# The first two column pairs of an input projection by plain products of quarters instead of seven products

## The chip, the cores and the metric

The kernel runs on one core of a Trainium2 chip. The metric is the device time of one execution in microseconds (us). Before the change it is 2447.02 us, the median of 3 runs (2444.62 to 2449.98). The profile is of one further execution, which took 2455.27 us.

The engines are named as in the profile: PE (TensorE, matrix products), PEld (its weight loads), DVE (VectorE), ACT (ScalarE), POOL (GpSimd) and SP (SyncE, which here issues the DMAs). Each engine takes its instructions in the order in which the program lists them.

## What is computed

One encoder block on a sequence of 2048 tokens of width 1024. The part that matters here is the first step: a pre-norm and one combined projection, whose columns feed all branches.

```python
h = rms_norm(x, norm_pre_g)
proj = jnp.einsum('bsd,de->bse', h, w_in.astype(h.dtype))
split_points = [int(p) for p in np.cumsum(SPLIT_SIZES)[:-1]]
u_a, z_a, q, k, v, o, z_b, gates, g_a, g_b = jnp.split(proj, split_points, axis=-1)
...
merged = jax.nn.sigmoid(g_a + b_merge[0]) * p_a + jax.nn.sigmoid(g_b + b_merge[1]) * p_b
```

Here x is 2048 x 1024 and w_in is 1024 x 9232. Of the columns, 16 are gate columns (`gates`), the other 9216 are 72 column blocks of 128. A pooling mixer and a matrix memory follow, then three more projections; they aren't touched by the change.

## The kernel before

**Halves and pairs.** `phase1` (L407) does the projection. It runs over two halves of the sequence with 1024 tokens each (`HALF`), and in each half over 36 pairs of column blocks (`in_pairs`, L48). The first two pairs are `("ga", 0)` and `("gb", 0)`, columns whose results only pass a sigmoid with a bias (`pair_g`, L653).

**Seven products.** A half of x, transposed, is a matrix of 1024 channels by 1024 tokens. It is cut into four quarters: A11 and A12 are the first 512 tokens (block 0) with the first and the last four of the eight k-tiles of 128 channels, A21 and A22 the same of the last 512 tokens (block 1). A pair's weights are cut alike: B11 and B21 are the first column block, B12 and B22 the second. `strassen` (L369) computes the four output quarters with seven products of quarters, the Winograd form. For it, the operands are A11, A12, A22 and the sums S1 = A21 + A22, S3 = A11 - A21, S2 = S1 - A11 and S4 = A12 - S2; the weights are B11, B21, B22 and the differences T1 to T4. Sums and differences are formed on DVE.

**Each product in three.** Every operand is split into a high part (ACT, L92) and a low part (DVE or POOL, L96). `mm3` (L98) does high by high, high by low and low by high for each of four k-tiles, so a product of quarters is 12 products on PE of 128x128 by 128x512. The seven take 84.

**Operands.** `operands` (L212) fetches x (L225). In half 0 it also forms the norm: squares on ACT (L246), their sum over k-tiles on DVE (L248), the sum over channels on PE (L252, tile `ssqp`), `rstd_of` (L146: DVE, then a power on POOL, L151), and `rows_of` (L167), which spreads the result over the partitions by PE (L173, tile `rbp`) and copies it to `rb` by ACT (L180). `scale_h` (L191, on DVE) scales x in place. `put` splits a k-tile into the tiles of `hp`, one buffer for each of A11, A12, S2, S1, S3, A22, S4. `combos` (L196) splits A22 and forms and splits S1, S3 and S2; S4 comes last (L208).

**Weights.** `load_w` (L301) loads raw weights into `wr` (3 buffers), `prep_w` (L341) forms the differences (L350, `wt`, 3 buffers) and splits everything into `wc` (16 buffers; a split matrix takes two). In half 1, `again_w` (L306) reads back differences that half 0 has stored, from the third pair on.

**The start of a half.** For the first two pairs and the last, `edge` is true (L446, L479): the product A12 by B21 comes right behind A11 by B11, since both need block 0 alone. The first two pairs run two steps each, then the gate columns of block 0 follow (`gates`, L513); then come the rest of the operands, the remaining products of both pairs, and the gate columns of block 1, which are formed from S1 and A22. In half 1 the operands are listed early by a priority of 400 instructions (`NEXT`); the x tiles 3 and 7 are first fetched as one block each and later fetched again whole.

**Order.** A planner with a cost model fixes the order of the instructions of each engine before the run, by priorities and by the times that it expects; `high_priority` raises the instructions traced inside it. `issue_after(i)` makes an instruction come behind `i` in the queue of the engine of `i`; instructions on other engines are not bound by it. Results in PSUM have two banks for each of `bankA`, `bankB`, `bankC` and `tr`.

Of the kernel before, what the change touches and what calls it, by code (L numbers as in the profile page):

```python
# [13 lines left out]
P = 128  # L14
# [63 lines left out]
class Kernel:  # L78
    def __init__(self, ctx, tc, a):
        self.ctx, self.tc, self.nc, self.a = ctx, tc, tc.nc, a  # L80
        self.n = 0
        self.free = {}
# [6 lines left out]
    def split(self, hi, lo, x, hi_eng, lo_eng):  # L89
        nc = self.nc  # L90
        if hi_eng == "act":
            nc.scalar.activation(hi, x, AF.Copy)  # L92
        else:
            nc.vector.tensor_copy(hi, x)
        eng = nc.gpsimd if lo_eng == "pool" else nc.vector
        eng.tensor_tensor(lo, x, hi.bitcast(F32), op=ALU.subtract)  # L96
# [70 lines left out]
    def rows_of(self, half, b, out, psum):  # L167
# [3 lines left out]
        for i in range(4):  # L171
            col = half * 8 + b * 4 + i
            nc.tensor.matmul(  # L173
# [6 lines left out]
        nc.scalar.activation(out, ps, AF.Copy)  # L180
# [7 lines left out]
    def put(self, H, n, j, x, he, le):  # L188
        self.split(H[n][0][:, j, :], H[n][1][:, j, :], x, he, le)

    def scale_h(self, x, kt, rb):  # L191
        self.nc.vector.scalar_tensor_tensor(
# [3 lines left out]
    def combos(self, H, j, a11, a12, a21, a22):  # L196

        nc = self.nc
        self.put(H, "A22", j, a22, "act", LE22)
# [12 lines left out]
    def operands(self, half, H, hp, wc, pool, psum):  # L212
# [3 lines left out]
        X = {}  # L216

        def whole(kt):
            x = pool.tile([P, HALF], F32, tag="raw" if kt < 4 else "acc", name=self.nm("xT"))
            X[kt] = x[:, :BLK], x[:, BLK:]  # L220
            return x

        def fetch(x, kt, b, n=1):
            t0 = half * HALF + b * BLK
            nc.sync.dma_start(x, a["xT"][kt, :, t0 : t0 + n * BLK])  # L225

        def parts(pool, tag, n):
            return tuple(pool.tile([P, BLK], F32, tag=tag, name=self.nm("xT")) for _ in range(n))

        last = []  # L230
        rb = self.rows.tile([P, HALF], F32, tag="rb", name=self.nm("rb"))
        if half == 0:
            for kt in range(KT):
                if kt % 4 == 3:
                    X[kt] = parts(wc, "wc", 2)
                else:
                    whole(kt)
            with tc.high_priority():
                for b in range(2):
                    for kt in range(KT):  # L240
                        fetch(X[kt][b], kt, b)
                for b in range(2):
                    acc = None
                    for kt in range(KT):
                        sq = pool.tile([P, BLK], F32, tag="p", name=self.nm("sq"))
                        nc.scalar.activation(sq, X[kt][b], AF.Square)  # L246
                        if acc is not None:
                            nc.vector.tensor_tensor(sq, sq, acc, op=ALU.add)  # L248
                        acc = sq
                    ps = psum.tile([P, 4], F32, tag="tr", name=self.nm("ssqp"), bufs=2)  # L250
                    for i in range(4):
                        nc.tensor.matmul(  # L252
                            ps[:, i : i + 1], acc[:, i * P : (i + 1) * P], self.one_c, start=True, stop=True
                        )
                    ssq = pool.tile([P, 4], F32, tag="ssq", name=self.nm("ssq"), bufs=2)
                    last = self.rstd_of(ssq, ps, 0, b)
                    self.rows_of(0, b, rb[:, b * BLK : (b + 1) * BLK], psum)
# [3 lines left out]
            yield  # L261
        else:
            for b in range(2):
                self.rows_of(1, b, rb[:, b * BLK : (b + 1) * BLK], psum)
            for kt in range(KT):
                if kt % 4 == 3:
                    X[kt] = parts(pool, "p", 1)
                    fetch(X[kt][0], kt, 0)
                else:
                    fetch(whole(kt), kt, 0, 2)  # L270
        H.update(self.alloc_h(hp))
        for kt in range(KT):
            with ExitStack() as es:
                if kt > 0:
                    for i in last:
                        es.enter_context(tc.issue_after(i.ins))
                self.scale_h(X[kt][0], kt, rb[:, :BLK])
                self.put(H, "A11" if kt < 4 else "A12", kt % 4, X[kt][0], "act", ("dve", "pool")[kt % 2])
        yield
        ends = []  # L280
        for j in range(4):
            for kt in (j, 4 + j):
                if len(X[kt]) == 1:
                    x = whole(kt)
                    fetch(x, kt, 0, 2)
                    self.scale_h(x, kt, rb)
                else:
                    self.scale_h(X[kt][1], kt, rb[:, BLK:])
            end = self.combos(H, j, X[j][0], X[4 + j][0], X[j][1], X[4 + j][1])
            if half == 1 and j == 0:  # L290
                end()
            else:
                ends.append(end)
# [3 lines left out]
    def put_w(self, W, wc, n, x, le):  # L297
        W[n] = tuple(wc.tile([P, 4, P], F32R, tag="wc", name=self.nm(f"w{n}{p}")) for p in "hl")
        self.split(*W[n], x, "act", le)

# [40 lines left out]
    def prep_w(self, W, raw, wc, wt):  # L341
# [11 lines left out]
        if "B11" not in W:  # L353
            put("B11", b11, "pool")
            if self.edge:
                put("B21", b21, "pool")
        yield
# [11 lines left out]
    def strassen(self, H, W, psum, pool, out, n=BLK, swap=False):  # L369


        nc = self.nc
        bank = {
# [32 lines left out]

    def phase1(self):  # L407
# [1061 lines left out]
```

## Time and profile before

| | us |
|---|---|
| median of 3 runs | 2447.02 |
| the profiled execution | 2455.27 |
| its span | 2453.5 |
| PE busy | 2331.6 |
| DVE busy | 1535.1 |
| POOL busy | 1141.2 |
| ACT busy | 902.0 |

The span runs from the first to the last instruction of the profiled execution; the rest of its time lies around that. A busy share is an average over the whole span. A product's end is modelled and products overlap, so the pace of PE is read from the starts of consecutive products, not from their durations. Idle time in a row is followed by what ended most of it. Lines are those of the kernel; L92, L96 and L104 to L106 are in helpers, so their rows are told apart by the tiles.

### The profile page before, as it was taken

How to read it: one execution, taken by the hardware profiler on the slowest of the kernel's cores; microseconds unless marked ns; L12 is line 12 of the kernel's file. 1: busy time of each engine (PE TensorE's matmuls, PEld its weight loads, DVE VectorE, ACT ScalarE, POOL GpSimd, SP SyncE). 2: the span in 40 equal slices, each digit the busy share in tenths (PEclk: the TensorE clock that was granted, in tenths of full speed). 3: DMA queues.
4: the chain of work that ended last, by engine and by line, in shares of the span. 5: the costliest groups of instructions: out<-in, count | busy, mean ns of one | idle time of the engine just before them, and what ended most of it. 6: DMA issues, size and time to landing. Idle time of an engine off the chain costs nothing. (4 is left out here: it accounts for less than half of the span.)

```text
span 2453.5 us, 35614 instructions
## 1 busy us (share of the span) xinstructions
PE 2331.6 (95%) x12517; PEld 2003.5 (82%) x12517; DVE 1535.1 (63%) x2540; ACT 902.0 (37%) x1781; POOL 1141.2 (47%) x902
## 2 busy tenths in 40 slices
PE   5899999999999889999999999998999999999898
PEld 3688788778778678888888888898989999999676
DVE  8787767796884655633554633887885333334885
ACT  5444433333434423321321323766664212111332
POOL 4556655565555423544454531444554211234675
PEclk9999999999999999999999999999999999999999
DMA  4456665555675366687767876767666546567443
GB/s 144 138 207 227 237 230 216 203 185 204 213 253 193 127 170 211 209 263 235 241 225 236 260 250 226 234 203 230 201 183 205 178 153 202 185 199 246 157 155 120
DMA packets 295874, 500.12 MB, mean 204 GB/s; under 512 B 26512, under 2 KB 139280, under 8 KB 295696
## 3 DMA queue, kind: packets, MB, share of 16 engines
q1 hardware_dynamic: 295696, 497.85, 61.6%
q8 instruction: 98, 1.61, 0.3%
q14 instruction: 80, 0.66, 0.1%
HBM read 308.49 MB, written 189.27 MB: 203 GB/s over the span
## 5 line engine op out<-in xcount | busy, mean ns | idle before, releaser
L565 DVE SCALAR_TENSOR_TENSOR acc<-raw,conv_w,acc 128x1022 f32<-128x1022 f32 (+1 forms) x128 | 212.1, 1677 | 13.0 <-ACT acc L561 12.4
L96 POOL TENSOR_TENSOR wB21l<-wraw,wB21h 128x512 fp32r<-128x512 f32 x76 | 115.3, 1517 | 188.0 <-ACT wB21h L92 131.0
L96 POOL TENSOR_TENSOR wB22l<-wraw,wB22h 128x512 fp32r<-128x512 f32 x76 | 109.7, 1443 | 113.1 <-ACT wB22h L92 82.6
L1117 POOL TENSOR_TENSOR qs<-q,isc 128x256 f32<-128x256 f32 x120 | 91.5, 766 | 138.0 <-PE num L1133 60.6
L841 PE MATMUL pb<-oxs,w_proj_mlstmh 128*128 128x256 f32 x512 | 143.7, 281 | 0.5 <-DVE sgb L1263 0.5
L843 PE MATMUL pb<-oxs,w_proj_mlstml 128*128 128x256 f32 x512 | 143.8, 281 | 0.0
L842 PE MATMUL pb<-oxs,w_proj_mlstmh 128*128 128x256 f32 x512 | 143.7, 281 | 0.0
L842 PE MATMUL paps<-pys,w_proj_poolh 128*128 128x256 f32 x512 | 143.1, 282 | 0.3 <-POOL pys L96 0.3
L841 PE MATMUL paps<-pys,w_proj_poolh 128*128 128x256 f32 x512 | 142.0, 282 | 0.3 <-DVE sga L970 0.3
L843 PE MATMUL paps<-pys,w_proj_pooll 128*128 128x256 f32 x512 | 141.9, 282 | 0.0
L96 POOL TENSOR_TENSOR wB11l<-wraw,wB11h 128x512 fp32r<-128x512 f32 x72 | 106.3, 1477 | 64.4 <-ACT wB11h L92 50.6
L104 PE MATMUL bankB<-A22h,wT4h 128*128 128x512 f32 x288 | 116.8, 405 | 17.6 <-DVE u L397 12.7
L397 DVE TENSOR_TENSOR u<-bankB,p 128x512 f32<-128x512 f32 x80 | 54.7, 683 | 117.4 <-PE bankB L106 117.4
L570 POOL TENSOR_TENSOR acc<-acc,raw 128x1022 f32<-128x1022 f32 (+1 forms) x32 | 82.9, 2590 | 91.0 <-ACT raw L569 76.2
L104 PE MATMUL bankB<-S3h,wT3h 128*128 128x512 f32 x288 | 114.3, 397 | 10.5 <-DVE u L393 10.5
L104 PE MATMUL bankC<-S1h,wT1h 128*128 128x512 f32 x288 | 113.6, 395 | 8.6 <-ACT S1h L92 7.1
L105 PE MATMUL bankA<-A11l,wB11h 128*128 128x512 f32 x288 | 114.2, 396 | 7.6 <-DVE A11l L96 6.0
L92 ACT ACTIVATE wB21h<-wraw 128x512 fp32r<-128x512 f32 x76 | 47.7, 628 | 195.3 <-PE bankA L105 87.1
L104 PE MATMUL bankB<-S2h,wT2h 128*128 128x512 f32 x288 | 112.8, 393 | 6.5 <-ACT S2h L92 6.5
L104 PE MATMUL bankA<-A12h,wB21h 128*128 128x512 f32 x288 | 113.3, 393 | 3.6 <-ACT p L386 3.6
L105 PE MATMUL bankB<-S2l,wT2h 128*128 128x512 f32 x288 | 113.4, 394 | 2.8 <-DVE S2l L96 2.8
L104 PE MATMUL bankC<-S4h,wB22h 128*128 128x512 f32 x288 | 112.9, 392 | 2.5 <-DVE u L635 2.5
(355 smaller groups left out, 7738.7 us busy)
## 6 DMA issues: line engine op xcount, KB each, us to landing
wraw<-in_w_in SPq DMA_DIRECT2D x112, 512.0 KB, 4.1
wt<-wT2h SPq DMA_DIRECT2D x34, 256.0 KB, 4.0
wt<-wT2l SPq DMA_DIRECT2D x34, 256.0 KB, 4.1
wt<-wT1h SPq DMA_DIRECT2D x34, 256.0 KB, 4.6
wt<-wT1l SPq DMA_DIRECT2D x34, 256.0 KB, 3.7
wt<-wT3h SPq DMA_DIRECT2D x34, 256.0 KB, 4.6
wt<-wT3l SPq DMA_DIRECT2D x34, 256.0 KB, 4.1
wt<-wT4h SPq DMA_DIRECT2D x34, 256.0 KB, 2.1
```

Of the source, the lines that this page charges most:

```text
L92: nc.scalar.activation(hi, x, AF.Copy)
L96: eng.tensor_tensor(lo, x, hi.bitcast(F32), op=ALU.subtract)
L104: nc.tensor.matmul(ps, wh, xh, start=start and kt == 0, stop=False, skip_group_check=True)
L105: nc.tensor.matmul(ps, wh, xl, start=False, stop=False, skip_group_check=True)
L397: nc.vector.tensor_tensor(u3, bank["B"], p1, op=ALU.add)
L565: nc.vector.scalar_tensor_tensor(acc[:, :n], raw[:, tap : tap + n], self.cw[:, ct, tap : tap + 1], acc[:, :n], op0=ALU.mult, op1=ALU.add,)
L570: nc.gpsimd.tensor_tensor(acc[:, :n], acc[:, :n], raw[:, :n], op=ALU.mult)
L841: nc.tensor.matmul(ps, wh, xh, start=i == 0, stop=False)
L842: nc.tensor.matmul(ps, wh, xl, start=False, stop=False)
L843: nc.tensor.matmul(ps, wl, xh, start=False, stop=i == n)
L1117: nc.gpsimd.tensor_tensor(qs[d], q[:, :, ck], isc[:, d, j % 2, None, :].to_broadcast([P, 2, P]), op=ALU.mult)
```

## The change

**Plain products for two pairs.** For the first two pairs of each half, `strassen` hands over to the new `quarters`. It takes the four output quarters one block at a time: for block u it has two banks, one for each column block, and adds up over the eight k-tiles three products for each bank. The two pairs and the gate columns advance together, a k-tile at a time. No sum and no difference is used. The last four banks go through `pair_g`'s `out` with nothing to add.

```diff
+    def quarters(self, H, W, psum, out):
+        nc = self.nc
+        for u, tags in enumerate(self.plain):
+            bank = [psum.tile([P, BLK], F32, tag=f"bank{t}", name=self.nm(f"bank{t}"), bufs=2) for t in tags]
+            for kt in range(KT):
+                xh, xl = (t[:, kt % 4, :] for t in H[f"A{u + 1}{1 + kt // 4}"])
+                es = ExitStack()
+                if u == 0 and kt == KT - 2 and self.half == 0:
+                    es.enter_context(self.tc.issue_after(self.ready[0].ins))
+                for e in range(2):
+                    wh, wl = (t[:, kt % 4, :] for t in W[f"B{1 + kt // 4}{1 + e}"])
+                    first, end = kt == 0, kt == KT - 1
+                    nc.tensor.matmul(bank[e], wh, xh, start=first, stop=False, skip_group_check=True)
+                    nc.tensor.matmul(bank[e], wl, xh, start=False, stop=False, skip_group_check=True)
+                    nc.tensor.matmul(bank[e], wh, xl, start=False, stop=end, skip_group_check=True)
+                es.close()
+                if kt < KT - 1:
+                    yield
+            with self.tc.issue_after(self.ready[1].ins):
+                for e in range(2):
+                    out(2 * u + e, bank[e], None)
+            yield
```

`ready` holds the last product of `rows_of` on PE and its copy to `rb` on ACT. So in half 0 the products of k-tile 6 of block 0 come behind block 1's `rbp` on PE, and the evacuations behind block 1's `rb` on ACT.

**Operands.** The blocks of x are fetched one behind the other, in half 0 with three raw weight loads between them. Tiles 3 and 7 of x lie in `wc`, which grows from 16 to 20 buffers, so nothing is fetched twice. All four quarters are split; A21 uses the buffer of S4. The norm of block 1 (`sums(1)`) is listed between k-tiles 1 and 2 of block 0's scaling, its instructions on DVE behind the second scaling, without a raised priority. The scaling of k-tile pairs is pinned behind the low part of the pair before. Two extra products (`busy`) go to PE in half 0 behind the sums of block 0.

```diff
+        def busy(w, x):
+            ps = psum.tile([P, BLK], F32, tag="bankC", name=self.nm("busy"), bufs=2)
+            nc.tensor.matmul(ps, w, x, start=True, stop=True)
...
+        scaled, lower = [], []
+        for b in range(2):
             for kt in range(KT):
+                if half == 0 and b == 0 and kt == 2:
+                    with tc.issue_after(scaled[1].ins):
+                        sums(1)
+                with ExitStack() as es:
+                    if kt > 0 and b == 0:
+                        for i in last if kt < 2 else lower[kt - 2 - kt % 2 :][:1]:
+                            es.enter_context(tc.issue_after(i.ins))
+                    scaled.append(self.scale_h(X[kt][b], kt, rb[:, b * BLK : (b + 1) * BLK]))
+                    lower.append(
+                        self.put(H, f"A{b + 1}{1 + kt // 4}", kt % 4, X[kt][b], "act", ("dve", "pool")[kt % 2])
+                    )
+            self.scaled = scaled
+            yield
+        ends = [self.combos(H, j, X[j][0], X[4 + j][0], X[j][1], X[4 + j][1]) for j in range(4)]
         yield
+        H.update(self.alloc_h({"S4": hp["S4"]}))
         for end in ends:
             end()
```

**The start of a half.** Both pairs' weights are split as they are, in four matrices each (`plain_w`). The sums S1 to S4 are now for the pairs from the third on. Their instructions on ACT are pinned behind the last evacuation of block 0; the differences of the third pair's weights, in half 0, are pinned on DVE behind the first scaling of block 1.

```diff
+                both = []
+                for i in range(2):
+                    self.plain = ("AB", ("CC", "AB")[i])
+                    both.append(work(i, W[i]))
+                    next(both[i])
+                self.plain = None
                 gates = self.gates(half, H, wg, psum, pool)
+                for _ in range(KT):
+                    next(gates, None)
+                    for g in both:
+                        next(g)
+                with tc.issue_after(self.evac.ins):
+                    next(ops)
...
                         if half == 0:
-                            run(self.prep_w(W, load(i), wc, wt))
+                            with tc.issue_after(self.scaled[8].ins) if i == 2 else ExitStack():
+                                self.prep_w(W, load(i), wc, wt)
```

**Gate columns.** Block 1's are formed from A21 and A22 with the weights as they are, so the difference of the gate weights goes; all eight k-tiles are split at once. The number of gate products, 16 for a block, stays.

200 lines of the change are left out of this document (87 added, 113 removed).

## The prediction

> **What bounds the kernel now.** I read the page first: its span, the row of TensorE (PE) and the row of its busy share in 40 slices. Then I cut the start into windows of 20 us.
>
> ```profile
> span 2453.5 us, 35614 instructions
> PE 2331.6 (95%) x12517; PEld 2003.5 (82%) x12517; DVE 1535.1 (63%) x2540; ACT 902.0 (37%) x1781; POOL 1141.2 (47%) x902
> PE   5899999999999889999999999998999999999898
> ```
>
> ```profile
> 0.00:20.00 20.00, 4.23 (x18) 3.88 (x18) 10.58 (x43) 11.91 (x19) 1.73 (x5) 1.00 0.84 274
> 20.00:40.00 20.00, 11.64 (x32) 8.09 (x32) 19.94 (x20) 8.57 (x16) 15.08 (x10) 0.96 0.27 84
> 40.00:60.00 20.00, 15.91 (x61) 9.76 (x59) 20.00 (x27) 11.79 (x19) 9.94 (x6) 0.95 0.24 80
> 60.00:80.00 20.00, 11.62 (x34) 7.04 (x35) 20.00 (x22) 7.65 (x13) 12.17 (x8) 0.74 0.01 3
> ```
>
> PE is busy 95% of the span and full from the third slice on, so the end of the kernel moves when work is taken from PE or a hole in PE is closed. In the windows (busy us and count for PE, PEld, DVE, ACT, POOL, then granted clock, DMA share, GB/s) the first 80 us are the hole: DVE has no idle time from 20 to 80 us while PE runs a third of what it could. VectorE, preparing operands, sets the pace there.
>
> How much is lost? The timeline gives PE's full pace (12 products lie between these two starts); the windows and the groups by line give what was done:
>
> ```profile
> 87.66 0.39 PE L104 MATMUL bankA<-A11h,wB11h 128*128 128x512 f32 x1
> 90.38 0.39 PE L104 MATMUL bankB<-A22h,wT4h 128*128 128x512 f32 x1
> ```
>
> ```profile
> 0.00:84.70 84.70, 47.86 (x160) 32.10 (x160) 73.04 (x114) 41.83 (x69) 41.18 (x30) 0.92 0.32 104
> 800.00:840.00 40.00, 29.83 (x109) 19.81 (x108) 34.50 (x38) 17.69 (x30) 21.66 (x15) 0.87 0.24 77
> ```
>
> ```profile
> L173 PE MATMUL rbp<-ident,rstd 128*128 128x128 f32 x16 | 4.2, 441 | 3.1 <-POOL rstd L151 3.1
> L252 PE MATMUL ssqp<-one_c,sq 128*128 128x1 f32 x16 | 3.7, 353 | 13.4 <-DVE sq L248 13.4
> ```
>
> Pace: (90.38 - 87.66)/12 = 0.227 us. By 84.7 us PE had done 160 records, of which 32 are the small ones of L173 and L252: 128 products, worth 29.1 us. **Half 0 is 84.7 - 29.1 = 55.6 us behind** a PE that never waits; from there on it runs without a gap for a while. At the start of half 1, 109 products fell into 40 us: 40 - 24.7 = **15.3 us behind**. The waits of PE name why:
>
> ```profile
> PE bankA L105 <- DVE A11l L96: 6.0, 2, 4.1
> PE bankB L104 <- ACT S2h L92: 3.5, 1, 3.5
> PE bankB L105 <- DVE S2l L96: 2.8, 1, 2.8
> ...
> PE bankC L104 <- ACT S1h L92: 6.9, 2, 5.9
> ```
>
> The first three are of the first 130 us, the last is of 800 to 840 us. Three of the four are waits for S1 or S2, the sums of quarters which only the seven-product scheme needs.
>
> **The change, part by part.**
>
> *More products.* A pair by seven products has 7 x 12 = 84, by plain products 8 x 12 = 96. Two pairs in each half: 24 more, 24 x 0.227 = 5.45 us a half. The 32 gate products of a half stay 32. Nothing hides this: PE is the bound.
>
> *Half 0: work for PE before the sums exist.* The two pairs and the gates now need only the scaled quarters, 224 products or 51 us. The chain to the first operand stays as it is:
>
> ```profile
> 13.13 1.87 PE L252 MATMUL ssqp<-one_c,sq 128*128 128x1 f32 x8 [13.13 <-DVE sq L248]
> 15.69 3.88 DVE L248 TENSOR_TENSOR sq<-sq,sq 128x512 f32<-128x512 f32 x5
> 15.74 1.53 POOL L151 TENSOR_TENSOR rstd<-ssq,half_c 128x4 f32<-128x4 f32 x1 [15.30 <-DVE ssq L149]
> 17.32 2.08 PE L173 MATMUL rbp<-ident,rstd 128*128 128x128 f32 x8 [2.32 <-POOL rstd L151]
> 20.06 0.75 DVE L192 SCALAR_TENSOR_TENSOR xT<-xT,norm_pre_g,rb 128x512 f32<-128x512 f32 x1 [0.50 <-ACT rb L180]
> 21.53 0.80 PE L104 MATMUL bankA<-A11h,wB11h 128*128 128x512 f32 x1
> 22.42 1.75 DVE L96 TENSOR_TENSOR A11l<-xT,A11h 128x512 fp32r<-128x512 f32 x1
> ```
>
> So PE starts its products at 21.5 us, as now. The two new "busy" products are not in this trace. By L173, 8 records of 128 columns take 2.08 us; one product of 512 columns (two records, four times as wide) is then 2 x 4 x 0.26 = 2.1 us. The first lies in the gap 15.0 to 17.3, the second between 19.4 and 21.5: bounds 0 and 4.2 us, taken as 0, since each gap is as long as it. POOL now has weight splits (1.47 us) queued before rstd, which may push the chain by up to one of them; that is in the stalls below.
>
> *Can the operands keep up?* One k-tile feeds 14 products, 3.2 us at full pace. The mean durations between 20 and 84 us (between 12 and 84 us for POOL):
>
> ```profile
> L192 DVE SCALAR_TENSOR_TENSOR xT<-xT,norm_pre_g,rb 128x512 f32<-128x512 f32 x16 | 16.2, 1060 | 0.5 <-ACT rb L180 0.5
> L203 DVE TENSOR_TENSOR xT<-xT,xT 128x512 f32<-128x512 f32 x4 | 4.6, 1215 | 0.0
> L202 DVE TENSOR_TENSOR xT<-xT 128x512 f32<-128x512 f32 x3 | 4.1, 1402 | 0.0
> L201 DVE TENSOR_TENSOR xT<-xT,xT 128x512 f32<-128x512 f32 x4 | 3.7, 953 | 0.0
> L96 DVE TENSOR_TENSOR S2l<-xT,S2h 128x512 fp32r<-128x512 f32 x4 | 3.7, 945 | 0.0
> ...
> L96 POOL TENSOR_TENSOR A11l<-xT,A11h 128x512 fp32r<-128x512 f32 x2 | 3.4, 1718 | 0.0
> L96 POOL TENSOR_TENSOR wB11l<-wraw,wB11h 128x512 fp32r<-128x512 f32 x2 | 2.9, 1466 | 3.4 <-ACT wB11h L92 3.4
> ```
>
> Two k-tiles cost DVE two scalings and one low part, about 3 us, and POOL one low part, 1.7 us, against 6.4 us of PE. Hence PE stays fed. DVE's list until the second quarter sum S2 is whole: 16 scalings 16.2, 8 low parts 8, 7 additions of squares at 0.78 to 1.75 (5.5 to 12, taken 7), gate weights 2, weight differences for the third pair 5, L201 3.7, L202 5.5 for four, L203 4.6, S2l 3.7: 56 us, from 20 to 76 us. PE asks for S2 after 224 + 12 products: 21.5 + 53.6 + 2 (cold clock, next) = 77. It is just in time; S4, eight operations later on DVE, is wanted 14 us later still. POOL's list to the same point, from 15 us on, is shorter: 13 weight splits at 1.47, 16 low parts at 1.72, two rstd at 1.53, 50 us, to 65.
>
> *The clock.* The first products run at half pace until PE has been full for a while:
>
> ```profile
> 39.04 0.80 PE L105 MATMUL bankA<-A11l,wB11h 128*128 128x512 f32 x1 [4.14 <-DVE A11l L96]
> 40.06 0.63 PE L104 MATMUL bankA<-A11h,wB11h 128*128 128x512 f32 x1
> 41.34 0.63 PE L104 MATMUL bankA<-A11h,wB11h 128*128 128x512 f32 x1
> 41.77 0.49 PE L105 MATMUL bankA<-A11l,wB11h 128*128 128x512 f32 x1
> 74.59 0.80 PE L105 MATMUL bankB<-S2l,wT2h 128*128 128x512 f32 x1 [2.77 <-DVE S2l L96]
> 79.45 0.43 PE L104 MATMUL bankB<-S2h,wT2h 128*128 128x512 f32 x1
> ```
>
> Three products from 40.06 to 41.34: 0.427 us each, and the full pace 2.7 us after 39.04 and 4.9 us after 74.59. At half pace a share of 1 - 0.227/0.427 = 0.47 is lost, so warming costs 1.3 to 2.3 us; taken 2.
>
> *Other stalls in half 0*, taken at 6 us: the first low part (0.9 to 2.7 us after the first product in the rows above), POOL's queue before k-tiles 4 to 7, the second block's sums (rbp is pinned ahead of k-tile 6), and S2. Below 0 isn't possible; the upper end is the rivals'. Half 0 is then behind by 21.5 + 2 + 6 = 29.5 us: 55.6 - 29.5 - 5.45 = **20.6 us gained**.
>
> *Half 1.* Block 0 works while the S4 buffer (now A21 too) is still read by half 0's last products; block 1 has 25 us of PE work as cover, and the third pair's sums 51 us. The second fetch of two x tiles, behind the 5.9 us wait for S1h, is gone since X keeps its tiles in the wider weight pool. I leave 3 us of the 15.3: 15.3 - 3 - 5.45 = **6.9 us gained** (bounds: 9.9 with no stall, 0 if 10 us stay).
>
> *DMA and SP.* The second block of x now queues behind three weight loads of 512 KB: 1.5 MB at the 274 GB/s of the first window, 5.7 us later. Now its squares and its rstd end so:
>
> ```profile
> 13.44 4.51 ACT L246 ACTIVATE sq<-xT 128x512 f32<-128x512 f32 x7 [0.33 <-DMA xT<-in_xT]
> 25.52 1.46 POOL L151 TENSOR_TENSOR rstd<-ssq,half_c 128x4 f32<-128x4 f32 x1 [1.90 <-DVE ssq L149]
> ```
>
> The squares would end near 23.7 instead of 18.0 us, still 19 us before k-tile 6 is issued (21.5 + 2 + 84 x 0.227 = 42.6). The evacuations pinned behind rb, and the sums' copies pinned behind the last evacuation of block 0, wait on ACT, which is under two thirds full in every window above; behind them on ACT stand only later splits. Cost 0; without that cover about 0.5 us each (8.57/16 in the second window).
>
> **Sum:** 20.6 + 6.9 = 27.5 us. Against the profiled execution's own 2455.3 us that is 2427.8; that execution stands 8.3 us above the median 2447.0 of the runs, so the forecast is 2447.0 - 27.5 = **2419.5, say 2420 us**.
>
> **Rivals.**
>
> 1. *PE is held at the pinned place.* If DVE does all of block 0 (8 scalings 8.1, 4 low parts 4, gates 2) before the 7 additions at 1.75 (12.3), these end at 46.5; with the sum on PE 1.9, POOL's queue and rstd 3.2, rbp 2.1 the place opens at 54, 11 us after 42.6, and PE cools: 2 more. Beyond my allowance that is 10 us: gain 17, 2430 us. For it: SP's new order delays these squares. Against: now the same chain is through at 27.0 (25.52 + 1.46). Chance 0.13.
>
> 2. *The clock stays at half pace through block 0.* Between 21.5 and 39 us PE is half busy and never speeds up; if the new start is as broken, 112 products at 0.427 end at 69.3 instead of 55: gain 13, 2434 us. Against it: 14 products a k-tile at half pace are 6 us, more than DVE needs, so PE would be full, which warmed it in at most 4.9 us above. Chance 0.1. The Trainium skill ("TensorE: Matmul & The Clock Gate", Part 1) says that the array runs at half clock until about 3.4 us of sustained activity and falls back after an idle window of that length. The 2.7 and 4.9 us above agree; by its figure my term of 2 us would be 1.6, an estimate, and any hole of over 3.4 us between blocks would cost that again.
>
> 3. *The sums are late after all.* With every two-input operation at 1.75 us, as A11l at 22.42, DVE's list takes 36 x 1.75 + 16.2 + 2 = 81 us and ends at 101, 24 us after S2 is wanted; of my allowance 2 us were for that, and PE cools once more, 2 us. Gain 3.5, 2443.5 us, no change that can be told. Against it: the means 0.95 to 1.4 us in the rows above. Chance 0.1.
>
> 4. *The rest of the phase pays.* The weight pool grows from 16 to 20 buffers and the order of the other 34 pairs of each half is planned anew; weight splits may run ahead of the evacuations on DVE for which PE already waits:
>
> ```profile
> PE bankB L104 <- DVE u L397: 11.9, 8, 4.3
> ```
>
> That is 1.5 us a wait, 8 times in the pairs from 95 to 1500 us. If most of the 34 pairs of half 0 had one (24 x 1.5 = 36 us), the kernel would be slower: 2447 - 27.5 + 36 = 2456; it decides from 22 such waits (27.5 + 4.9 = 32.4 us). Against it: the raw and difference buffers (3 and 3) stay and hold the planner back as now. Chance 0.08.
>
> That the change doesn't do what it says is excluded for the main step: the sums read scaled quarters, so they can't come ahead of them.
>
> **How the numbers follow.** Forecast 0.59, rivals 0.13, 0.1, 0.1, 0.08. The low end is all allowances gone: 20.6 + 6 + 6.9 + 3 = 36.5, so 2411; the high end takes in rivals 1 to 3: 2444. A measurement here tells 0.2%, 4.9 us, from no change. Faster by more: forecast and rivals 1 and 2, 0.82; within: rival 3, 0.1; slower: rival 4, 0.08.
>
> **What would show it.** Right: PE without a gap over 3 us from 21.5 to about 80 us, the clock full by 28 us, some 115 more products done by 84.7 us ((84.7 - 29.5)/0.227 = 243 against 128), no wait for S1h or S2h over 2 us in either half. Wrong: a wait of PE for rstd (L151) or rbp near 43 us (rival 1), products 0.427 us apart past 30 us (rival 2), a wait for S2h or S2l near 77 us (rival 3), more waits for L397 between 100 and 700 us (rival 4).

## The result, and the profile after

The changed kernel takes 2437.41 us (median, 2430.06 to 2438.41) where the kernel before takes 2447.02: a ratio of 0.995 with a 95% interval of 0.9939 to 0.9962, so 9 to 15 us less. The forecast was 2420 us, 27.5 us less. The sign is right; more than half of the gain is missing. The profiled execution of the changed kernel took 2438.41 us.

The page of the changed kernel, its span, the busy times and PE's row of slices:

```profile
span 2436.6 us, 35625 instructions
...
PE 2335.1 (96%) x12569; PEld 2008.3 (82%) x12569; DVE 1505.3 (62%) x2495; ACT 894.3 (37%) x1773; POOL 1148.2 (47%) x902
...
PE   7999899999999999999999999998999999999898
```

The first slice went from 5 to 7, and the dent in slices 14 and 15 (the start of half 1) is gone. A new 8 stands in slice 5, at 244 to 305 us, where the change touches nothing. The windows say how much (columns as in the prediction: busy us and count for PE, PEld, DVE, ACT, POOL, then granted clock, DMA share, GB/s):

```profile
0.00:81.20 81.20, 64.11 (x260) 47.96 (x261) 60.72 (x89) 41.16 (x67) 43.76 (x33) 0.96 0.36 122
81.20:105.00 23.80, 18.04 (x65) 13.74 (x64) 19.64 (x23) 10.94 (x20) 14.84 (x10) 0.86 0.71 255
800.00:840.00 40.00, 40.00 (x176) 31.21 (x175) 29.44 (x32) 19.45 (x36) 26.41 (x16) 1.00 0.34 114
```

The third pair begins at 81.2 us. Of the 260 records before that, 36 are the small ones and the busy ones, so 224 products: PE is 81.2 - 224 x 0.227 = 30.4 us behind, where it was 55.6 us behind. At the start of half 1, 176 products fill all 40 us: nothing is left of 15.3 us. Both are what the prediction's sum needed. But the second row is new. The kernel before ran this stretch without a hole:

```profile
81.20:105.00 23.80, 23.47 (x104) 19.09 (x103) 14.03 (x16) 9.81 (x17) 12.11 (x9) 1.00 0.61 202
```

Now it holds 65 products instead of 104, and 23.8 - 65 x 0.227 = 9.0 us are lost as soon as the new start is over. A third place is the long middle of half 0. Its window, first of the kernel before, then of the changed one:

```profile
105.00:790.00 685.00, 663.76 (x2911) 543.68 (x2910) 513.61 (x562) 263.30 (x427) 388.69 (x238) 0.99 0.61 217
```

```profile
105.00:790.00 685.00, 656.93 (x2869) 537.07 (x2868) 508.54 (x556) 258.34 (x420) 384.96 (x236) 0.98 0.60 214
```

PE does 42 products less in the same 685 us: 9.5 us. The ends of the projection come from the last S4 product in the listing of tile wB22h (first and last start stand behind the durations), before and after:

```profile
L104 PE MATMUL bankC<-S4h,wB22h x288: 387/389/628, 94.0 to 1520.5; 128*128 128x512 f32 x144
```

```profile
L105 PE MATMUL bankC<-S4h,wB22h x272: 389/389/500, 111.8 to 1506.7; 128*128 128x512 f32 x136
```

| of the profiled executions | before, us behind | after, us behind | difference |
|---|---|---|---|
| start of half 0, to the third pair | 55.6 | 30.4 | -25.2 |
| third pair, 81.2 to 105 us | 0.2 | 9.0 | +8.8 |
| middle of half 0, 105 to 790 us | 24.2 | 33.7 | +9.5 |
| start of half 1 | 15.3 | 0 | -15.3 |
| 48 more products of 0.227 us | | | +10.9 |
| sum | | | -11.3 |
| measured at the end of the projection | 1520.5 | 1506.7 | -13.8 |

The 55.6 us are counted to 84.7 us; by 81.2 us they are 55.1, so the sum is uncertain by 0.5 us. The 2.5 us left over lie in the rest of half 1, where the changed kernel does 11 products more between 840 and 1500 us. The spans differ by 16.9 us, but the profiled execution of the kernel before was one of its longest; by the ratio the gain is 12.2 us. The table names two losses that the forecast did not have, 8.8 and 9.5 us. The experiments are about these two.

### The profile page after: what moved, and what is told of

It reads as the page before. It is cut to its first block, busy times and chain, and to the rows that moved or that the text cites. A ratio compares the mean times of both kernels' runs of the same rounds, so it can differ in the third digit from the quotient of the medians.

```text
span 2436.6 us, 35625 instructions
## 1 busy us (share of the span) xinstructions
PE 2335.1 (96%) x12569; PEld 2008.3 (82%) x12569; DVE 1505.3 (62%) x2495; ACT 894.3 (37%) x1773; POOL 1148.2 (47%) x902
## 4 chain that ended last, share of the span: by engine, by line
PE 51%; DMA 10%; DVE 6%; issue 2%; POOL 1%; ACT 1%; SPq 0%; DVEq 0%; POOLq 0%; ACTq 0%
PE bankB L105 5%; PE bankB L107 5%; PE bankB L106 4%; PE num L1167 4%; PE bankC L105 3%; PE bankC L107 3%; PE bankC L106 3%; PE bankA L107 3%; PE bankA L106 3%; PE bankA L105 3%; PE paps L876 2%; PE paps L877 2%; PE paps L875 2%; DMA negM<-nm 1%; DVE o L1392 1%
## 5 line engine op out<-in xcount | busy, mean ns | idle before, releaser
L599 DVE SCALAR_TENSOR_TENSOR acc<-raw,conv_w,acc 128x1022 f32<-128x1022 f32 (+1 forms) x128 | 212.4, 1688 | 10.9 <-ACT acc L595 8.8
L97 POOL TENSOR_TENSOR wB22l<-wraw,wB22h 128x512 fp32r<-128x512 f32 x76 | 115.6, 1521 | 91.0 <-ACT wB22h L93 53.5
L105 PE MATMUL bankB<-A22h,wT4h 128*128 128x512 f32 x272 | 111.9, 411 | 23.5 <-DVE u L400 23.5
L400 DVE TENSOR_TENSOR u<-bankB,p 128x512 f32<-128x512 f32 x76 | 52.0, 684 | 108.7 <-PE bankB L107 108.7
L105 PE MATMUL bankB<-S3h,wT3h 128*128 128x512 f32 x272 | 108.4, 398 | 7.9 <-DVE u L396 7.9
L105 PE MATMUL bankC<-S1h,wT1h 128*128 128x512 f32 x272 | 107.2, 394 | 3.4 <-ACT sg L700 3.4
L107 PE MATMUL bankB<-A22h,wT4l 128*128 128x512 f32 x272 | 109.7, 403 | 0.0
L106 PE MATMUL bankB<-A22l,wT4h 128*128 128x512 f32 x272 | 109.5, 403 | 0.0
L105 PE MATMUL bankC<-S4h,wB22h 128*128 128x512 f32 x272 | 106.3, 391 | 1.5 <-DVE u L669 0.8
L106 PE MATMUL bankB<-S3l,wT3h 128*128 128x512 f32 x272 | 107.3, 394 | 0.0
L107 PE MATMUL bankB<-S3h,wT3l 128*128 128x512 f32 x272 | 107.2, 394 | 0.0
L107 PE MATMUL bankC<-S1h,wT1l 128*128 128x512 f32 x272 | 107.2, 394 | 0.0
```

The costliest lines, as they stand in the source:

```text
L97: return eng.tensor_tensor(lo, x, hi.bitcast(F32), op=ALU.subtract)
L105: nc.tensor.matmul(ps, wh, xh, start=start and kt == 0, stop=False, skip_group_check=True)
L106: nc.tensor.matmul(ps, wh, xl, start=False, stop=False, skip_group_check=True)
L107: nc.tensor.matmul(ps, wl, xh, start=False, stop=stop and kt == 3, skip_group_check=True)
L400: nc.vector.tensor_tensor(u3, bank["B"], p1, op=ALU.add)
L599: nc.vector.scalar_tensor_tensor(acc[:, :n], raw[:, tap : tap + n], self.cw[:, ct, tap : tap + 1], acc[:, :n], op0=ALU.mult, op1=ALU.add,)
```

## The first loss: an evacuation behind a split

PE's waits of the changed kernel between 82 and 106 us (us in total, times, longest), then ACT's and PE's timelines around the longest. `sg` is an evacuation of a bank by ACT, `u` is an addition on DVE that reads a finished bank (L393 and L397 in the kernel before, L396 and L400 in the changed one); PE's next product into that bank waits for it. The wait put down to `raw` L589, a small fill, is before a product with T2's low part, which DVE ends in the same moment.

```profile
PE bankC L105 <- ACT sg L700: 3.4, 1, 3.4
PE bankB L105 <- DVE u L396: 1.2, 1, 1.2
PE bankB L107 <- DVE raw L589: 1.2, 1, 1.2
```

```profile
84.46 0.61 ACT L93 ACTIVATE wB21h<-wraw 128x512 fp32r<-128x512 f32 x1
89.89 0.63 ACT L93 ACTIVATE wT4h<-wt 128x512 fp32r<-128x512 f32 x1 [4.82 <-DVE wt L352]
90.43 0.61 ACT L93 ACTIVATE wB22h<-wraw 128x512 fp32r<-128x512 f32 x1
90.95 0.67 ACT L700 ACTIVATE sg<-bankC,b_merge 128x512 f32<-128x512 f32 x1
```

```profile
87.92 0.39 PE L107 MATMUL bankB<-S2h,wT2l 128*128 128x512 f32 x1
91.67 0.80 PE L105 MATMUL bankC<-S1h,wT1h 128*128 128x512 f32 x1 [3.36 <-ACT sg L700]
92.26 0.63 PE L106 MATMUL bankC<-S1l,wT1h 128*128 128x512 f32 x1
```

The four banks of block 1 are complete when the third pair starts, and the third pair needs them empty. The evacuation of the first (sg) takes 0.67 us, and ACT is idle. But in ACT's list it stands behind the split of T4, and that split waits 4.82 us for a difference from DVE, which is still busy with the low parts of S2 and S4. So ACT idles with the evacuation in its queue, PE stands for 3.4 us, and comes back at half pace (starts 0.43 us apart) until 96.95 us. The Trainium skill ("TensorE: Matmul & The Clock Gate", "Architectural detail") says that ACT and DVE take their instructions strictly first in, first out, and that only PE may pull something ahead; these rows agree, with 4.82 us.

**e1: T4 and B22 of the third pair are split behind the last evacuation of block 1.**

```diff
-        put("T4", diff(b21, t2), "pool")
-        put("B22", b22, "pool")
+        with self.tc.issue_after(late.ins) if late is not None else ExitStack():
+            put("T4", diff(b21, t2), "pool")
+            put("B22", b22, "pool")
...
-                                self.prep_w(W, load(i), wc, wt)
+                                self.prep_w(W, load(i), wc, wt, self.evac if i == 2 else None)
```

> The third pair's last two weight splits (T4, B22) are pinned on ACT behind the last evacuation of block 1 in half 0; all else is the changed kernel. Theory: PE lost 9.3 us between 81 and 105 us (its lag behind full pace went from 30.6 to 39.9) because block 1's four sigmoid evacuations stood on ACT behind the split of T4, which waited for DVE, and the third pair's product S1 by T1 needs one of their banks. Then the 3.4 us wait of bankC for sg goes, the clock doesn't drop at 91 us, the lag at 105 us is 32 to 34, and the kernel is 5 to 8 us faster than the changed one (about 2430 us against 2437). Rival: DVE's list is the bound there, and the next thing from it (T2l, S4l, u) is late anyway; then the lag at 105 us stays above 37 and the time within 3 us of the changed kernel's.

Measured: 2434.53 us, ratio 0.994 (0.9923 to 0.9957). ACT's timeline, PE's longest wait and the window of e1:

```profile
84.66 1.25 ACT L701 ACTIVATE sg<-bankC,b_merge 128x512 f32<-128x512 f32 x2
85.80 0.69 ACT L701 ACTIVATE sg<-bankA,b_merge 128x512 f32<-128x512 f32 x1
...
89.58 0.64 ACT L93 ACTIVATE wT4h<-wt 128x512 fp32r<-128x512 f32 x1 [2.51 <-DVE wt L352]
...
92.15 0.57 ACT L390 ACTIVATE p<-bankA 128x512 f32<-128x512 f32 x1
```

```profile
PE bankA L105 <- ACT p L390: 2.1, 1, 2.1
```

```profile
81.20:105.00 23.80, 20.61 (x82) 15.96 (x80) 20.87 (x22) 12.30 (x22) 16.73 (x11) 0.93 0.80 281
```

The wait for sg is gone: the evacuations run at 84.66 to 87 us, while T4 still waits. The stretch holds 82 products instead of 65, so 3.9 us less are lost in it. PE is 35 us behind at 105 us, between the 34 of the theory and the 37 of the rival. The time moves by about 2.5 us, less than the 5 to 8 that were expected, and an amount that the intervals of the two kernels don't separate. What is late next stands in the same rows: the third pair's own first copy (p, L390) is behind five weight splits on ACT, and PE waits 2.1 us for it. The mechanism is shown; the pin alone is worth little, because the next instruction of the same queue takes its place.

## The second loss: four more weight buffers

**e2: the kernel before with 20 weight buffers, nothing else.**

```diff
-            wc = es.enter_context(tc.tile_pool(name="wc", bufs=16))
+            wc = es.enter_context(tc.tile_pool(name="wc", bufs=20))
```

> The kernel before with 20 instead of 16 buffers for split weights and nothing else. Theory: the deeper pool lets weight splits run ahead of evacuations on DVE in the other 34 pairs of half 0, which cost the changed kernel 8 to 9 us (gaps of PE between 105 and 790 us 30.0 against 22.2, waits for the u of L397 20.7 against 11.9); then this kernel has gaps near 30 there and is 5 to 9 us slower than the kernel before. Rival: depth does nothing by itself, the other start alone moved the planned order; then the gaps stay at 20 to 24 and the time within 3 us of the kernel before.

Measured: 2467.38 us, ratio 1.0075 (1.0058 to 1.0093): **slower by 18 us**, with no change to the start at all. PE's waits between 105 and 790 us, of the changed kernel and of e2:

```profile
PE bankB L105 <- DVE u L400: 20.7, 10, 4.7
PE bankB L105 <- DVE u L396: 4.6, 3, 4.2
```

```profile
PE bankB L104 <- DVE u L397: 22.0, 10, 4.7
```

```profile
105.00:790.00 685.00, 655.22 (x2854) 535.35 (x2853) 503.40 (x556) 258.13 (x420) 376.74 (x234) 0.98 0.60 215
```

The kernel before with 20 buffers waits as the changed kernel does: ten waits of 2.1 to 2.2 us each, and 29.8 us of idle PE in this window (685 - 655.22) against 28.1 and, with 16 buffers, 21.2. The kernel before has 11.9 us in 8 waits for `u` L397, and a ninth of 4.7 us before the same kind of product, which its profile puts down to a small fill (L578) that ended in the same moment. So long waits for `u` were there before; with 20 buffers there are more. The two kernels with 20 buffers start differently and yet have nearly the same waits one behind the other (4.74 and 4.73, 1.26 and 1.26, 4.24 and 4.24, 2.02 and 2.02, 2.72 and 2.71 us).

The longest wait that the kernel before hasn't got shows what stands ahead of `u` on DVE, first in e2 with PE's wait, then in the kernel before at the same place of its order:

```profile
733.51 1.76 DVE L350 TENSOR_TENSOR wt<-wraw,wt 128x512 f32<-128x512 f32 x1 [3.70 <-POOL wT1l L96]
...
739.43 1.75 DVE L350 TENSOR_TENSOR wt<-wraw,wt 128x512 f32<-128x512 f32 x1
741.10 1.74 DVE L192 SCALAR_TENSOR_TENSOR xT<-xT,norm_pre_g,rb 128x512 f32<-128x512 f32 x1
742.76 0.68 DVE L393 TENSOR_TENSOR u<-bankB,p 128x512 f32<-128x512 f32 x1
```

```profile
743.50 0.80 PE L104 MATMUL bankB<-S3h,wT3h 128*128 128x512 f32 x1 [4.49 <-DVE u L393]
```

```profile
722.90 0.68 DVE L393 TENSOR_TENSOR u<-bankB,p 128x512 f32<-128x512 f32 x1
...
728.32 0.68 DVE L350 TENSOR_TENSOR wt<-wraw,wt 128x512 f32<-128x512 f32 x1
```

In e2 the last product into the bank starts at 731.01 us, and `u` comes over 11 us later. Ahead of it in DVE's queue stands a difference of the next pair's weights that waits 3.70 us for POOL, and behind that more differences and the scalings of half 1's x. With 16 buffers the difference comes 5.4 us behind `u`. The changed kernel has the same wait: its difference at 716.45 us waits 3.70 us for POOL, `u` follows at 720.38, and PE stands for 4.15 us. It is the first loss again, in another queue. That the plan moves the weight work because a buffer is free earlier fits the edit; no row shows the planner's reason.

The 18 us of e2 aren't in the middle alone. Against the kernel before it does 57 products less between 105 and 790 us (12.9 us), 26 less between 81.2 and 105 us (5.9 us) and 19 less between 840 and 1500 us (4.3 us), but 27 more from 800 to 840 us (6.1 us).

**e7: the changed kernel with 16 weight buffers; x tiles 3 and 7 get four buffers of their own.**

```diff
-                X[kt] = tuple(wc.tile([P, BLK], F32, tag="wc", name=self.nm("xT")) for _ in range(2))
+                X[kt] = tuple(xw.tile([P, BLK], F32, tag="xw", name=self.nm("xT")) for _ in range(2))
...
-            wc = es.enter_context(tc.tile_pool(name="wc", bufs=20))
+            wc = es.enter_context(tc.tile_pool(name="wc", bufs=16))
+            xw = es.enter_context(tc.tile_pool(name="xw", bufs=4))
```

> The changed kernel with the split-weight pool back at 16 buffers; the four x tiles that had lain in it get a pool of their own with 4 buffers, so the start of each half has what it had. Theory: 20 buffers let the planner put the next pair's weight work ahead of evacuations on DVE; with 16 the gaps of PE between 105 and 790 us fall from 30.0 to 20 to 24, the waits for the u of L400 from 20.7 to about 12, and the kernel is 6 to 12 us faster than the changed one, about 2428 us. Rival: any new order of the start brings such gaps; then they stay at 28 or more and the time within 3 us of the changed kernel's 2437.

Measured: 2425.91 us, ratio 0.9918 (0.9902 to 0.9935). Its waits for `u` and its window:

```profile
PE bankB L105 <- DVE u L400: 11.4, 7, 4.3
```

```profile
105.00:790.00 685.00, 665.93 (x2937) 545.43 (x2936) 526.24 (x568) 268.60 (x435) 397.79 (x244) 0.99 0.60 214
```

The waits are back at 11.4 us, PE's idle time at 19.1, and the kernel is about 8 us faster than the changed one by the ratios, 11.5 by the medians. So the depth of the pool, not the plain products, makes the second loss. The middle now has 68 products more than in the changed kernel (15.4 us) and 26 more than in the kernel before.

The depth also had a part in the first loss. The stretch behind the new start in e7, and PE's longest wait in it:

```profile
81.20:105.00 23.80, 18.89 (x76) 14.59 (x75) 19.03 (x21) 11.23 (x21) 14.28 (x10) 0.93 0.88 295
```

```profile
PE bankA L105 <- ACT p L389: 3.8, 1, 3.8
```

Without the pin of e1 the wait for sg is gone: with 16 buffers the plan itself puts the first evacuation (86.17 us) ahead of T4's split (91.09 us). The stretch holds 76 products instead of 65, and a wait of 3.8 us for the copy `p` takes the place. So the two losses aren't independent.

**e10: the kernel before with 14 buffers**, to see whether shallower is better still.

```diff
-            wc = es.enter_context(tc.tile_pool(name="wc", bufs=16))
+            wc = es.enter_context(tc.tile_pool(name="wc", bufs=14))
```

> The kernel before with 14 instead of 16 buffers for split weights, as many as one pair fills. Theory: the depth sets how far the planner runs the next pair's weight work ahead; with 14 the gaps of PE between 105 and 790 us fall below 22.2 us or stay, and the kernel is within 5 us of the kernel before or faster. Rival: the cost of 20 buffers was one unlucky order and not a matter of depth; then 14 gives an order as bad, with gaps of 28 us or more, or starves PE of weights, and is over 5 us slower.

Measured: 2463.12 us, ratio 1.0065 (1.0051 to 1.0078), slower by 16 us. In the middle of half 0 PE is idle for 19.9 us, hardly less than with 16, and does 24 products more (5.4 us). In half 1 it does 49 products less between 840 and 1500 us (11 us). A weight that comes late is one reason, as this wait of PE there shows:

```profile
PE bankA L104 <- ACT wB11h L92: 3.0, 1, 3.0
```

The last S4 product starts 5.9 us later than before (1526.4 against 1520.5). The rest is lost behind the projection, where this pool isn't used: from that product to the last `num` product of the matrix memory it takes 335.7 us (to 1862.1) against 329.4 (to 1849.9). These 6.3 us are lost at once: in the first 40 us behind the projection PE does 174 records against 246, at a granted clock of 0.83 against 1.00, and it waits 4.4 us for the DMAs of `kT` and `q`, for which the kernel before doesn't wait there. Why they come later was not found. In the kernel before, 16 is better than either neighbour tried, but not for one reason that a rule could state.

## The two starts by themselves

**e3: the new start in half 1 alone. e4: in half 0 alone.** Both keep the old start, with its sums and its second fetch, in the other half; both have 20 buffers.

```diff
+                if half == 1:
                     ops = self.operands(half, H, hp, wc, pool, psum)
...
+                else:
+                    ops = self.operands_b(half, H, hp, wc, pool, psum)
```

(e4 has `half == 0` in the first line.)

> Half 0 starts as in the kernel before, half 1 as in the changed kernel, 20 weight buffers, gate weights split in both ways. Theory: half 1 alone brings what the two traces show for it, a lag of 0.5 instead of 15.7 us at its start less 5.45 us of added products, so about 10 us; 2437 us if the middle of half 0 is as in the kernel before, 2445 if the 20 buffers are what slows that middle by 9 us. Rival: half 1's gain hangs on half 0's changed order; then the lag at its start stays over 6 us and the gain is under 4 us.

> Half 0 starts as in the changed kernel, half 1 as in the kernel before, 20 weight buffers. Theory: half 0's start gains 25.4 us of lag, pays 5.45 us for its products and loses 9.3 us again in the third pair; that leaves 10.6 us if the middle of half 0 is as in the kernel before (2436 us) and 1 to 2 us if the loss of 9 us there comes with half 0's start or the buffers (2445 us). Rival: the loss in the middle comes from half 1's early fetches, which this kernel has in the old form; then the gaps between 105 and 790 us are near 22 us again and the time is near 2436 us.

Measured: e3 2457.3 us, ratio 1.0036 (1.0022 to 1.0051); e4 2452.5 us, ratio 1.0011 (0.9999 to 1.0023). The start of half 1 in e3, then in e4:

```profile
800.00:840.00 40.00, 40.00 (x176) 31.17 (x175) 31.46 (x38) 19.11 (x35) 23.34 (x15) 1.00 0.27 89
```

```profile
800.00:840.00 40.00, 32.52 (x123) 21.74 (x121) 30.35 (x34) 14.02 (x24) 18.44 (x12) 0.90 0.32 101
```

176 products against 123: each start does in its half what it does in the whole change. Against the kernel before neither alone is a gain, and both are slower than either time that was expected, since the 20 buffers cost the old kernel 18 us and not 8 to 9. In e4 the window from 105 to 790 us holds 2868 products, as in the changed kernel, so the loss there doesn't come from half 1's early fetches, its rival. Against e2, which pays for the same 20 buffers, half 1's start gains 0.0039 of 2447, 9.5 us (the table: 15.3 - 5.45 = 9.9), and half 0's 0.0064, 15.7 us. The table has 25.2 - 8.8 - 5.45 = 11 for half 0 with the third pair, but e2 is short of products between 81.2 and 105 us already: e4 has 66 there and e2 78, so only 2.7 of the 8.8 us count against e2. The parts make 18.4 - 9.5 - 15.7 = -6.8 us, and the change measures -12.2; each ratio is uncertain by 3 to 4 us, so this difference isn't shown to be real. The 20 buffers cost 18 us in the old kernel and some 8 to 11 in the new one.

**e5: the changed kernel without the two busy products.**

```diff
-            if b == 0:
-                busy(acc[:, :P], acc)
...
-            if b == 0:
-                busy(self.rstd[:, :1].to_broadcast([P, P]), acc)
```

> The changed kernel without the two busy products at the start of half 0. Theory: they lie in idle time of PE and only warm its clock; without them the first products run at 0.427 us for 3 to 6 us instead of 3, PE's lag at 40 us is 26 to 27 instead of 24.8, and the kernel is 0 to 3 us slower than the changed one, no more. Rival: they hold up rbp or the first product; then the first product starts before 21.4 us and the lag at 40 us is under 24.5.

Measured: 2439.39 us, ratio 0.9973 (0.9962 to 0.9984). The first 40 us of the changed kernel and of e5:

```profile
0.00:40.00 40.00, 24.13 (x90) 18.43 (x90) 26.37 (x57) 20.84 (x34) 19.12 (x17) 0.96 0.61 205
```

```profile
0.00:40.00 40.00, 19.24 (x71) 15.36 (x71) 25.91 (x57) 21.07 (x34) 18.75 (x17) 1.00 0.62 205
```

Without the small records (22 with the busy ones, 16 without) these are 68 and 55 products: PE is 24.6 and 27.5 us behind. So the busy products give about 3 us in the start; the 5.6 us between the two ratios may hold more, but the intervals meet. The prediction had counted them as neither cost nor gain.

**e6: the kernel before once more**, to see how far one profile of it can be trusted.

> The kernel before, unchanged, for a second profile: the first one is of an execution 8 us above its median. Theory: the start of half 0 and the order are fixed, so the lags at 85 us (56.0) and between 800 and 840 us (15.7) come again within 1 us, and the difference lies elsewhere in the first phase or behind it. Rival: the start itself varies by several us from run to run; then the sum of steps is uncertain by as much.

Measured: 2450.72 us, span 2448.9. By 85 us PE is 54.8 us behind (55.6 in the first profile), at half 1's start 15.0 (15.3), and in the window from 105 to 790 us it does 2911 products in both. The places of the table reproduce within a microsecond; the span differs by 4.6 us.

## A version without the two losses

**e8: e7 with the pin of e1.**

> As e7, and the third pair's T4 and B22 splits pinned behind block 1's last evacuation on ACT as in e1. Theory: both losses are apart, so this is 2 to 4 us faster than e7, about 2425 us, 22 us less than the kernel before and near the 27.5 us that were forecast. Rival: the pin only moved the wait to the next late thing and the planner gives it back; then it is within 2 us of e7.

Measured: 2424.13 us, ratio 0.9912 (0.9894 to 0.9929), not to be told from e7, as its rival has it. PE's longest wait after the new start is the one that took over in e1:

```profile
PE bankA L105 <- ACT p L390: 2.5, 1, 2.5
```

**e9: e8, and the weights of the fourth pair are prepared behind that first copy; p gets six buffers instead of five.**

```diff
-        nc.scalar.activation(p1, bank["A"], AF.Copy)
+        self.first = nc.scalar.activation(p1, bank["A"], AF.Copy)
...
-                        shape, dt, tag=tag, name=name, bufs=bufs or (5 if tag == "p" else 3)
+                        shape, dt, tag=tag, name=name, bufs=bufs or (6 if tag == "p" else 3)
...
-                            with tc.issue_after(self.scaled[8].ins) if i == 2 else ExitStack():
+                            with tc.issue_after((self.scaled[8] if i == 2 else self.first).ins) if i < 4 else ExitStack():
```

> As e8, with the fourth pair's weight splits pinned on ACT behind the third pair's copy of its first product (L390), and six instead of five buffers in the pool of small tiles that this copy and block 1's four sigmoid results share. Theory: what is left of the loss in the third pair (lag 31.0 at 85 us, 36.7 at 105 us in e8) is PE waiting for that copy, 2.5 us, and the cooling clock; then the lag at 105 us falls to 33 to 35 and the kernel is 1 to 4 us faster than e8, about 2422 us. Rival: the copy still stands behind T4's split, which waits for DVE until 89 us; then the lag at 105 us stays within 1 us of 36.7 and the time within 2 us of e8's 2424.

Measured: **2419.05 us, ratio 0.9884 (0.9871 to 0.9898)**, 28 us less than the kernel before and faster than every other version here. Its windows and its waits between 82 and 106 us:

```profile
81.20:105.00 23.80, 20.11 (x86) 15.63 (x85) 20.27 (x24) 10.73 (x19) 14.78 (x10) 1.00 0.86 299
105.00:790.00 685.00, 664.96 (x2942) 544.56 (x2941) 519.80 (x572) 266.65 (x433) 394.52 (x242) 1.00 0.60 214
```

```profile
PE bankB L105 <- DVE u L397: 1.6, 1, 1.6
PE bankB L107 <- DVE raw L591: 1.1, 1, 1.1
PE bankA L105 <- ACT p L390: 1.0, 1, 1.0
```

No wait is over 1.6 us, and the clock stays full (1.00 against 0.86); 86 products fit where the changed kernel has 65, and the middle of half 0 has 2942 against 2869. The copy's pin and the sixth buffer were not tried apart. This version lands on the forecast of the change: the gain of the starts was there, and two side effects hid most of it. That the number agrees so well is partly luck. The third pair's stretch is still 18 products (4.1 us) short of the kernel before, and the middle of half 0 has 31 products (7.0 us) more than the kernel before, which the forecast didn't count on.

## Why the prediction was right or wrong

- **What bounds the kernel, and the main step: right.** The start was worth what the prediction took for it. Half 0's start is 30.4 us behind, forecast 29.5, although its parts shifted. The first product starts at 21.47 us (forecast 21.5). The cold clock came twice, some 1.5 us each (forecast 2 once). PE idles 1.05 us for the second block's sums. One reading was too low: from 20 to 80 us of the kernel before PE did some 110 products, 42% of full pace and not "a third of what it could"; a third holds for the first 84.7 us.
- **Half 1: right, and better than forecast.** 0 us left where 3 were kept; the bound of no stall was the true one.
- **"Cost 0" for the evacuations on ACT: the first failed step.** The prediction took ACT's share of busy time as cover and wrote that "behind them on ACT stand only later splits". It asked what stands behind the evacuations, for block 0 alone, and not what stands ahead of those of block 1. A split that waits 4.82 us for DVE was ahead of them, on an idle engine. With what follows on the same queue and on DVE the third pair's stretch lost 8.8 us. Taking the split out of the way gave 3.9 us of them back in e1; with 16 buffers and the copy moved forward too, e9 got 4.8 us back.
- **DVE's list, "56 us, from 20 to 76 us": too short, the reason why the split was late.** The work was about as long as worked out, but the list had no wait in it. DVE stood for 7.0 us between 20 and 85 us, nearly all of it here, before the first scaling of block 1:

```profile
47.01 7.47 DVE L193 SCALAR_TENSOR_TENSOR xT<-xT,norm_pre_g,rb 128x512 f32<-128x512 f32 x8 [5.95 <-ACT rb L181]
```

Rival 1 asked only whether PE is held by the second block's sums; they held DVE. S2's last low part ends at 85.1 us instead of 76, and T4's difference starts at 89.12. PE asks for S2 at 84.0 us instead of 77, since the 6 us of stalls were left out of that sum, so that S2 was in time by luck: both sides were late alike. Seven us earlier T4's split would have been done before PE needs the bank at 88 us; that is an estimate from these rows, and no run tried it.

- **Rival 4, "The rest of the phase pays": the second failed step.** Its mechanism was real and its chance of 0.08 too small. The sentence against it, that the raw and difference buffers "stay and hold the planner back as now", is wrong: e2 changes the depth alone and has the longer waits, e7 takes the depth back and loses them. The sum had put this at nothing; it cost 9.5 us in the middle of half 0, and by e7 8 to 11 us in all. That is below the rival's 36: ten waits of 2.1 us, not twenty-four more of 1.5. A mechanism that didn't reach its turning point still took a third of the gain.
- **Rivals 1, 2 and 3 fell.** The second block's rbp starts at 42.2 us, when the prediction has k-tile 6 due (42.6), after 0.3 us of waiting for rstd; the first half pace ends at 25.7 us, before 28; and no product waits for S1h, S2h or S2l. Rival 2's sign, products 0.427 us apart past 30 us, does appear from 42.46 to 46.10 us, but not its mechanism: the pace is full from 25.9 us until the second block's sums.
- **The busy products** were right as a cost (nothing) and wrong as an effect: about 3 us of gain were not counted.

In sum, the two starts gave what was forecast, and the third pair and the middle of half 0 took more than half of it back: 27.5 forecast, plus 2.1 from the two starts (less 0.9 in half 0, 3 more in half 1), less 8.8 in the third pair, less 9.5 in the middle of half 0, is 11.3; measured 12.2 by the ratio.

## What to carry to other kernels

A busy share is no cover for an instruction in an ordered queue: look at what stands ahead of it there, and at what that waits for. When a tile borrows a place in a shared pool, the depth of the pool changes for everything else that uses it; give the tile a pool of its own, or time the new depth alone before the rest of the change. And after a wait has been taken away, read the same stretch again at once: e1 removed 3.4 us and met the next 2.1 us in the same queue.

## What the runs showed of the hardware

**Short holes cost a clock.** PE's timeline of the changed kernel at its first products:

```profile
18.45 1.18 PE L258 MATMUL busy<-sq,rstd 128*128 128x512 f32 x2
21.47 0.51 PE L423 MATMUL bankA<-A11h,wB11h 128*128 128x512 f32 x1 [1.84 <-ACT A11h L93]
...
22.36 0.63 PE L424 MATMUL bankB<-A11h,wB12l 128*128 128x512 f32 x1
...
25.34 0.51 PE L425 MATMUL bankA<-A11l,wB11h 128*128 128x512 f32 x1
25.70 0.40 PE L425 MATMUL bankB<-A11l,wB12h 128*128 128x512 f32 x1
```

After a hole of 1.84 us the first products start 0.24 to 0.34 us apart; 0.9 us later the pace halves, for 3.0 us. The same happens around the second block's sums: between the products that start at 38.40 and 40.72 us PE has only an idle 1.05 us and eight one-column products, and from 42.46 to 46.10 us its products are 0.43 us apart. In the middle of half 0, holes of 2.27 us (to 175.98 us) and 2.24 us (to 253.66 us) are followed by 7 and 8 products at half pace, and one of 2.02 us (to 607.06 us) by none. So holes well under 3 us can bring the drop and need not, and in these rows it comes 0 to 1.7 us behind their end. What decides is not shown. The Trainium skill ("TensorE: Matmul & The Clock Gate", Part 1) gives about 3.4 us for the idle window and says that this window runs freely; the pace of 0.427 us is the one that it states for a cold array, but the holes here were shorter than its figure.

**The granted clock doesn't show the first cold stretch.** In e5 the column says 1.00 for the first 40 us, while its products from 22.64 to 26.48 us start 0.43 us apart. The pace is read from the starts.

**What stays open:** why with 14 buffers the matrix memory's operands come later, why the planner moves weight work ahead of `u` with 20 and why their price differs by kernel, and how much of e9's last 5 us belongs to the pin and how much to the sixth buffer.
